# A two-layer trunk on one core: low halves of two weight chunks on VectorE, a longer distance between row sums, spread and turned row, odd heads' scores one product later, and values scaled in blocks

## The chip, the core and the metric

The kernel runs on one NeuronCore of a Trainium2 chip. The metric is the device time of one execution in microseconds (us); the time before is the median of three runs.

## What is computed

The reference has two decoder layers on a sequence of 512 tokens with 1024 channels. Both end in a SwiGLU feed-forward block; the first mixes tokens with dilated window attention in three head groups of eight heads, the second with a pooling mixer. The change touches the attention layer alone:

```python
def rmsnorm(x, g):
    y = xf * lax.rsqrt(jnp.mean(xf * xf, axis=-1, keepdims=True) + RMS_EPS)
    return (y * g.astype(jnp.float32)).astype(x.dtype)
...
    qkv = (h @ w_qkv).astype(jnp.float32).reshape(B, S, N_ATTN_GROUPS, 3, HEADS_PER_GROUP, HEAD_DIM)
...
    s = jnp.einsum('bnqhd,bnkhd->bnhqk', qb, kb) * (D ** -0.5)
    s = s + bias[None, None]
    p = jnp.exp(s - m)
    den = jnp.sum(p, axis=-1, keepdims=True)
    o = jnp.einsum('bnhqk,bnkhd->bnqhd', p / den, vb)
...
    wts = jax.nn.softmax(jnp.stack(lses, axis=0), axis=0)
    o = jnp.sum(wts[..., None] * o, axis=0).reshape(B, S, ATTN_WIDTH)
    return o.astype(h.dtype) @ w_out
```

## The kernel before

**High and low parts.** Every matrix operand is split into a high part in the type fp32r and a low part, the rest, and a product is three matmuls: high by high, high by low, low by high. `split` (lines 90 to 92) lets ScalarE write the high part and VectorE the low one by a subtraction. A plain chunk of weights (class `Plain`) can instead be "lean" (lines 144 to 148): ScalarE writes the high part, then its negative into the low part's place, and GpSimd issues a transfer that reads the chunk from HBM a second time and adds it there. Two chunks at the start, those of the third head group's query and key of head 0 (`w_qk`, line 241), are lean.

**Seven products.** Most other weights come as `Pair` units: Strassen's scheme with seven half-size products in place of eight. `Pair.load` (line 165) starts three loads on the SP queue (L169, L170, L171) and one on GpSimd's queue that adds a quarter onto the loaded first buffer (L172, line 172). The steps `blocks`, `sums`, `more` and `last` then split the parts "b", "s", "m" and "l"; `more` first makes its sums on VectorE (L188, L189), and every split has its high part at L91 on ScalarE and its low part at L92 on VectorE. Part "s" is made of the buffer onto which the accumulating transfer adds, so it cannot be split before that transfer lands. Loads stand in buffers `raw` (four) and `rawhalf` (two), split weights in `w` (five) and `half` (two); `pump` starts a load or split when its buffers are free. `seven` (line 465) computes such a unit (L456 to L458), `values12` (line 618) the values of two head groups for two heads at once (L632 to L634), and between their products run hooks, "behind(i)".

**The start.** A loop over eight blocks of channels loads input and first weights, and runs 96 matmuls (L927) for the first four query and key tiles. Meanwhile ScalarE and VectorE add up the squares of the input (L377, L379). Then, in the order of lines 930 to 970: `begin` starts the product of the first lean chunk with two of its eight blocks of channels; `prepare(0)` makes the sums of the input that Strassen's scheme wants (L576, L582 to L587, splits at L91 and L92); `rstd` (line 399) sums the squares over channels on TensorE (L406), forms the variance on VectorE (L409) and its power -1/2 on GpSimd in two halves (L412, tile `rcol`); `spread` (line 415) multiplies that column by an identity, so that every partition gets the row (L419, copied to `row` at L939); ScalarE reorders the row (L942, tile `line`) and four one-column matmuls turn it into columns (L944), from which and from `rcol` the scales `rk` are made (L946, L948). The eight blocks of the first lean chunk's product stand as two before the sums, three before the spread and three before the turned row; the whole product of the second chunk comes after. `evac` (line 608) moves the finished query and key tiles out (L613, L615).

**The heads.** Each head after the first computes its queries and keys by three calls of `seven`; an even head then computes the values of the first group by another call, an odd head those of the two other groups by `values12`. Hooks place the rest: `scores0` and `scores12` (scores of the first and of the two other groups), `scatter` and `merge` (one softmax over the groups), `turn0`, `turn12` (transposes of the weights), `output` (L843). `scores12` of an odd head reads the last key tile that L513 writes at the end of the third `seven`, and stands behind the first product of `values12`. At its end, `values12` scales the four blocks (classes) of its result by `rk` on ScalarE (L680), in four whole blocks.

**What sets the order.** The program is recorded and a scheduler orders each engine's instructions by its own estimates; on the chip each engine runs its list in that order and waits in place. So the order below is that of the built programs.

Of the kernel before, what the change touches and what calls it, by code (L numbers as in the profile page):

```python
# [18 lines left out]
KC = D // P  # L19
# [45 lines left out]
def trunk(ctx: ExitStack, tc: tile.TileContext, xT, xN, norms, w_first, w_qk, w_qkp, w_v0p, w_v12, w_out, w_outp, w_pair, w_down, w_dblock, w_pin, w_pgrp,  # L65
# [172 lines left out]

    for h in range(HEADS):
        if h == 0:  # L240
            plain(*[w_qk[u] for u in range(len(QK) - NF)], lean=True)
        for g in range(3):
            if h:
                pairs(w_qkp[3 * h - 3 + g])
        if h % 2 == 0:
            pairs(w_v0p[h // 2])
        else:
            pairs(w_v12[h // 2, 0], w_v12[h // 2, 1], shift=APART)
# [351 lines left out]
    with tc.tile_pool(name="opool", bufs=1) as opool:  # L600
        with tc.tile_pool(name="apool", bufs=1) as apool:
# [16 lines left out]
            def values12(after={}):  # L618


                t = apool.tile([P, NT, 4 * P], F32, name="v12")
                unit, = units.popleft()

                def product(name, half, key):
                    p = ps()
                    for a in range(2):
                        for k in range(K2):
                            wh, wl = (v[:, half * S + k % 2 * H2:half * S + (k % 2 + 1) * H2]
                                      for v in part(unit[k // 2], name).t)
                            mh, ml = (blk(v, a) for v in T[key, k])  # L630
                            o = both(p)[:, a]
                            nc.tensor.matmul(o, mh, wh, start=k == 0, stop=False)  # L632
                            nc.tensor.matmul(o, mh, wl, start=False, stop=False)  # L633
                            nc.tensor.matmul(o, ml, wh, start=False, stop=k == K2 - 1)  # L634
                        pump()
                    return p

                def done(name):
                    for u in unit:
                        u.w[name].done()  # L640

                def behind(i):
                    for f in after.get(i, ()):
                        f()

                def quarter(a, c):
                    return t[:, 2 * a:2 * a + 2, c * H2:(c + 1) * H2]

                m1 = product("b", 0, "11")
                first = scratch("first")  # L650
                nc.scalar.copy(first, m1)
                behind(0)
                m2 = product("b", 1, "21")
                nc.vector.tensor_add(quarter(0, 0), both(m2), both(first))
                done("b")
                behind(1)
                m5 = product("s", 0, "1")
                behind(2)
                m7 = product("s", 1, "3")
                done("s")  # L660
                behind(3)
                m6 = product("m", 0, "2")
                u2 = scratch("sums")
                nc.vector.tensor_add(u2, m6, first)
                u3 = scratch("sums")
                nc.vector.tensor_add(u3, m7, u2)
                nc.vector.tensor_sub(quarter(1, 1), both(m5), both(u3))
                behind(4)
                m3 = product("m", 1, "22")
                done("m")  # L670
                rest = scratch("first")
                nc.vector.tensor_add(rest, m3, u2)
                nc.vector.tensor_sub(quarter(1, 0), both(rest), both(m5))
                behind(5)
                m4 = product("l", 0, "4")
                done("l")
                nc.vector.tensor_sub(quarter(0, 1), both(m4), both(u3))
                behind(6)
                for r in range(NT):
                    nc.scalar.activation(t[:, r], t[:, r], AF.Copy, scale=rk[:, 1, r:r + 1])  # L680
                return t

            VT = []
# [246 lines left out]
            square(0, KC - 1)  # L930
            nc.sync.dma_start(ident, ident_in)
            nc.sync.dma_start(const[:, :3 * G + P], consts[:, :3 * G + P])
            lead += begin(1, 0, range(2))
            prepare(0)
            rcol = rstd([acc[0]])
            lead[-1].add(range(2, 5))
            rows["row"] = apool.tile([P, S], F32, tag="row", name="row")
            rk = apool.tile([P, NT, NT], F32, name="rk")
            nc.scalar.activation(rows["row"], spread(rcol), AF.Copy)  # L939
            lead[-1].add(range(5, KC))  # L940
            p, line = ps(), scratch("line")
            nc.scalar.copy(line[:1].rearrange("p (x y z) -> p x y z", y=Y16, z=2), in_a_row(rows["row"][:1]))  # L942
            for b in range(NT):
                nc.tensor.matmul(p[:, b:b + 1], blk(line, b)[:1], ones[:1], start=True, stop=True)  # L944
            for i, scale in ((0, 1.0), (2, SCALE)):
                nc.scalar.activation(rk[:, i], p[:, :NT], AF.Copy, scale=scale)  # L946
                for t, c in enumerate(rcol):
                    nc.scalar.activation(rk[:, i + 1, t:t + 1], c, AF.Copy, scale=scale)  # L948

            def later(f, *a):  # L950
                return lambda: f(*a)
# [11 lines left out]
            for u in range(NF):  # L963
                evac(0, u, lead[u].p)
            prepare(2)
            lead += begin(1, 0, range(KC))
            prepare(3)
            for u in range(NF, len(QK)):
                evac(0, u, lead[u].p)
# [2 lines left out]
            for h in range(HEADS):  # L972
                for g in range(3 if h else 0):
                    for c in range(2):
                        QKV[h, g, c] = apool.tile([P, S], F32, name=f"qk{g}{c}")
                    seven(T, QKV[h, g, 0], QKV[h, g, 1], scratch, between(h, g), g == 0, rows["row"])
                if h == 1:
                    O = [opool.tile([P, 2, S], F32, tag=f"o{k}", name="o") for k in range(K2)]
                    o.extend(O[h % K2][:, h // K2] for h in range(HEADS))
                if h % 2 == 0:  # L980
                    VT[:] = [apool.tile([P, n], F32, tag=tag, name="vt")[:, :S] for tag, n in (("room", 2 * S), ("o0", S))]
                    seven(T, *VT, scratch, {0: [] if h else [later(scores0, h)], 3: [later(scores12, h)],
                                            6: [later(scatter, h)]}, True)
                elif h < HEADS - 1:
                    QKV[h // 2, 12, 2] = values12({0: [later(scores12, h)], 4: [later(scatter, h)]})
                else:
                    QKV[h // 2, 12, 2] = values12({0: [later(scores12, h)], 1: [later(halve, 0), later(halve, 1)],
                                                   2: [later(scatter, h), later(halve, 2), later(halve, 3)],
                                                   3: [later(merge, h)],
                                                   4: [later(give, ("t", k, 0)) for k in range(2)]  # L990
                                                   + [later(halve, 4), later(halve, 5)]})
# [527 lines left out]
```

## Time and profile before

| What | Value |
|---|---|
| median of three runs | 1200.92 us |
| the runs | 1200.90, 1200.92 and 1203.81 us |
| the profiled execution | 1201.55 us |
| span of its instructions | 1199.8 us |
| mean granted TensorE clock | 0.996 |
| TensorE (PE) busy | 1180.0 us, 98% |
| weight loads (PEld) busy | 1125.4 us, 94% |
| VectorE (DVE) busy | 993.6 us, 83% |
| ScalarE (ACT) busy | 753.5 us, 63% |
| GpSimd (POOL) busy | 174.4 us, 15% |
| DMA, mean | 176 GB/s |

PE, PEld, DVE, ACT and POOL are the profile's names for TensorE's matmuls, its weight loads, VectorE, ScalarE and GpSimd; SPq and POOLq are the queues that issue transfers. In the views below a row of the timeline gives start, duration, engine, line, operation, the tiles written and read, their shapes, and in brackets the idle time before with what ended it. A row of the view of waits gives the total, the number and the longest of the waits. L327 is line 327. One execution was profiled; the 1.75 us of it outside the span lie before the first or after the last instruction.

### The profile page before, as it was taken

What the parts mean: (1) busy time and instruction counts of PE and PEld (TensorE: products, weight loads), DVE (VectorE), ACT (ScalarE), POOL (GpSimd) and SP (SyncE); (2) the same over time, 40 slices, a digit from 0 to 9 for tenths busy, and PEclk for the clock granted to TensorE, in tenths of its full rate; (3) what the DMA queues carried; (4) which work ended last, traced back from release to release, by engine and by line L of the source; (5) the groups of instructions that cost most, each with busy time, mean ns of one, the idle gap of its engine ahead of it and who ended that gap; (6) DMA issues with size and microseconds to landing.
All of it is one profiled execution on the core that took longest, in us unless ns stands there. A gap on an engine that the chain in (4) does not pass through costs nothing.

```text
span 1199.8 us, 25528 instructions
## 1 busy us (share of the span) xinstructions
PE 1180.0 (98%) x10158; PEld 1125.4 (94%) x10158; DVE 993.6 (83%) x1745; ACT 753.5 (63%) x1343; POOL 174.4 (15%) x170
## 2 busy tenths in 40 slices
PE   8899999999999999999999999999999999999997
PEld 7699999999999989889999999988888999999997
DVE  6698888889878979599988998755879998898875
ACT  8574655647556567657766775685574775677653
POOL 2121111111121001311111111121131111111100
PEclk9899999999999999999999999999999999999999
DMA  8666666766666464976777777698685777777732
GB/s 278 157 158 163 166 154 153 167 169 141 167 179 149 138 205 118 256 154 164 193 195 200 191 194 195 188 270 213 146 179 105 197 192 191 198 202 190 193 98 71
DMA packets 85304, 211.00 MB, mean 176 GB/s; under 512 B 7984, under 2 KB 13248, under 8 KB 85184
## 3 DMA queue, kind: packets, MB, share of 16 engines
q1 hardware_dynamic: 53104, 145.63, 36.6%
q0 software_dynamic: 31792, 63.46, 31.8%
q8 instruction: 79, 1.29, 0.4%
q14 instruction: 41, 0.34, 0.1%
q10 hardware_dynamic: 288, 0.29, 0.1%
HBM read 207.24 MB, written 2.10 MB: 174 GB/s over the span
## 4 chain that ended last, share of the span: by engine, by line
PE 83%; DVE 7%; DMA 6%; issue 2%; ACT 1%; POOL 1%; DVEq 0%; SPq 0%; POOLq 0%; ACTq 0%
PE ps L456 19%; PE ps L458 18%; PE ps L457 18%; PE ps L324 6%; PE ps L327 6%; PE ps L325 6%; DMA raw<-w_v 2%; PE ps L843 2%; DVE w L92 2%; PE ps L632 2%; PE ps L634 2%; PE ps L633 2%; DMA raw<-w_v0p 1%; DMA raw<-w_outp 1%; DVE half L92 1%
## 5 line engine op out<-in xcount | busy, mean ns | idle before, releaser
L91 ACT ACTIVATE w<-raw 128x1024 fp32r<-128x1024 f32 x269 | 285.4, 1063 | 185.0 <-PE ps L458 89.1
L92 DVE TENSOR_TENSOR w<-raw,w 128x1024 fp32r<-128x1024 f32 x269 | 328.5, 1223 | 55.2 <-ACT w L91 50.9
L456 PE MATMUL ps<-far,w 128*128 128x256 f32 x896 | 246.5, 275 | 0.0
L457 PE MATMUL ps<-far,w 128*128 128x256 f32 x896 | 246.5, 275 | 0.0
L458 PE MATMUL ps<-far,w 128*128 128x256 f32 x896 | 246.4, 275 | 0.0
L456 PE MATMUL ps<-near,w 128*128 128x256 f32 x749 | 210.9, 282 | 0.0
L458 PE MATMUL ps<-near,w 128*128 128x256 f32 x749 | 207.0, 276 | 0.0
L457 PE MATMUL ps<-near,w 128*128 128x256 f32 x749 | 206.9, 276 | 0.0
L456 PEld LDWEIGHTS ps<-far,w 128*128 128x128 f32 x896 | 168.2, 188 | 0.1
L457 PEld LDWEIGHTS ps<-far,w 128*128 128x128 f32 x896 | 168.2, 188 | 0.1
L458 PEld LDWEIGHTS ps<-far,w 128*128 128x128 f32 x896 | 168.2, 188 | 0.0
L456 PEld LDWEIGHTS ps<-near,w 128*128 128x128 f32 x749 | 140.7, 188 | 0.5
L457 PEld LDWEIGHTS ps<-near,w 128*128 128x128 f32 x749 | 140.8, 188 | 0.0
L458 PEld LDWEIGHTS ps<-near,w 128*128 128x128 f32 x749 | 140.8, 188 | 0.0
L327 PE MATMUL ps<-near,w 128*128 128x512 f32 (+1 forms) x332 | 126.1, 380 | 5.3 <-DMA w<-w_qk 5.3
L324 PE MATMUL ps<-near,w 128*128 128x512 f32 (+1 forms) x332 | 127.0, 383 | 0.0
L325 PE MATMUL ps<-near,w 128*128 128x512 f32 (+1 forms) x332 | 125.7, 378 | 0.0
L172 POOL DMA_DIRECT2D raw<-w_pair x36 | 43.6, 1210 | 293.7 <-DMA raw<-w_pair 135.3
L327 PEld LDWEIGHTS ps<-near,w 128*128 128x128 f32 x332 | 62.8, 189 | 17.4 <-DMA w<-w_qk 5.7
L325 PEld LDWEIGHTS ps<-near,w 128*128 128x128 f32 x332 | 63.0, 190 | 11.5 <-DVE near L92 0.2
L324 PEld LDWEIGHTS ps<-near,w 128*128 128x128 f32 x332 | 62.8, 189 | 11.6 <-ACT near L91 0.4
L188 DVE TENSOR_TENSOR raw<-raw 128x512 f32<-128x512 f32 x87 | 59.5, 684 | 10.7 <-DMA raw<-w_v0p 7.8
(340 smaller groups left out, 2739.3 us busy)
## 6 DMA issues: line engine op xcount, KB each, us to landing
raw<-w_pair SPq DMA_DIRECT2D x80, 512.0 KB, 4.9
raw<-w_qkp SPq DMA_DIRECT2D x42, 512.0 KB, 4.7
raw<-w_pair POOLq DMA_DIRECT2D x36, 512.0 KB, 7.6
raw<-w_dblock SPq DMA_DIRECT2D x32, 512.0 KB, 4.7
raw<-w_qkp POOLq DMA_DIRECT2D x21, 512.0 KB, 7.7
rawhalf<-w_pair SPq DMA_DIRECT2D x36, 256.0 KB, 5.1
raw<-w_v SPq DMA_DIRECT2D x16, 512.0 KB, 4.2
raw<-w_dblock POOLq DMA_DIRECT2D x16, 512.0 KB, 7.5
```

The costliest lines, as they stand in the source:

```text
L91: nc.scalar.activation(hi, v, AF.Copy)
L92: nc.vector.tensor_tensor(lo, v, hi.bitcast(F32), op=OP.subtract)
L172: nc.gpsimd.dma_start(self.b.rearrange("p (a c) -> p a c", a=2), self.src[:, None, 3 * n:].to_broadcast([P, 2, n]), accum_op=OP.add)
L188: nc.vector.tensor_add(a[:, :n], a[:, :n], b[:, :n])
L324: nc.tensor.matmul(self.p[:, cols], w[0][:, s], mh[:, cols], start=self.done == 0, stop=False)
L325: nc.tensor.matmul(self.p[:, cols], w[0][:, s], ml[:, cols], start=False, stop=False)
L327: nc.tensor.matmul(self.p[:, cols], w[1][:, s], mh[:, cols], start=False, stop=self.done == self.n)
L456: nc.tensor.matmul(dst, w.t[0][:, c], th, start=k == 0 and not on, stop=False, skip_group_check=on)
L457: nc.tensor.matmul(dst, w.t[0][:, c], tl, start=False, stop=False, skip_group_check=on)
L458: nc.tensor.matmul(dst, w.t[1][:, c], th, start=False, stop=k == n - 1, skip_group_check=on)
L632: nc.tensor.matmul(o, mh, wh, start=k == 0, stop=False)
L633: nc.tensor.matmul(o, mh, wl, start=False, stop=False)
```

## The change

It has four parts.

1. The two chunks of `w_qk` are no longer lean: their low parts come from a subtraction on VectorE (L92), and the two accumulating transfers (L148) go.
2. At the start the sums of squares (L406) come directly behind the 96 matmuls, then the whole product of the first chunk (24 matmuls), the spread, six of eight blocks of the second chunk's product (18 matmuls), the turned row and the last two blocks (6 matmuls). No product of a whole chunk is left behind the turned row.
3. In odd heads `scores12` and `scatter` move one product further on; in the last head `scatter` and `merge` stay where they were, and two of the splits of finished heads (`halve`) change places.
4. `values12` scales its result in smaller pieces as they are ready: the first half of the columns of blocks 0 and 1 and the whole of blocks 2 and 3 ahead of the last product, the second half of blocks 0 and 1 behind it.

```diff
-            plain(*[w_qk[u] for u in range(len(QK) - NF)], lean=True)
+            plain(*[w_qk[u] for u in range(len(QK) - NF)])
...
+                def scale(classes, c, n=1):
+                    for r in classes:
+                        v = t[:, r, c * H2:(c + n) * H2]
+                        nc.scalar.activation(v, v, AF.Copy, scale=rk[:, 1, r:r + 1])
...
                 behind(5)
+                scale(range(NT // 2), 0)
+                scale(range(NT // 2, NT), 0, 2)
                 m4 = product("l", 0, "4")
...
-                for r in range(NT):
-                    nc.scalar.activation(t[:, r], t[:, r], AF.Copy, scale=rk[:, 1, r:r + 1])
+                scale(range(NT // 2), 1)
...
-            lead += begin(1, 0, range(2))
+            rcol = rstd([acc[0]])
             prepare(0)
-            rcol = rstd([acc[0]])
-            lead[-1].add(range(2, 5))
+            lead += begin(1, 0, range(KC))
             rows["row"] = apool.tile([P, S], F32, tag="row", name="row")
             rk = apool.tile([P, NT, NT], F32, name="rk")
             nc.scalar.activation(rows["row"], spread(rcol), AF.Copy)
-            lead[-1].add(range(5, KC))
-            p, line = ps(), scratch("line")
+            line = scratch("line")
             nc.scalar.copy(line[:1].rearrange("p (x y z) -> p x y z", y=Y16, z=2), in_a_row(rows["row"][:1]))
+            lead += begin(1, 0, range(6))
+            p = ps()
             for b in range(NT):
                 nc.tensor.matmul(p[:, b:b + 1], blk(line, b)[:1], ones[:1], start=True, stop=True)
...
+            lead[-1].add(range(6, KC))
...
             prepare(2)
-            lead += begin(1, 0, range(KC))
             prepare(3)
...
-                    QKV[h // 2, 12, 2] = values12({0: [later(scores12, h)], 4: [later(scatter, h)]})
+                    QKV[h // 2, 12, 2] = values12({1: [later(scores12, h)], 5: [later(scatter, h)]})
                 else:
-                    QKV[h // 2, 12, 2] = values12({0: [later(scores12, h)], 1: [later(halve, 0), later(halve, 1)],
+                    QKV[h // 2, 12, 2] = values12({0: [later(halve, 0)], 1: [later(scores12, h), later(halve, 1)],
```

Lines behind the change have other numbers in the changed kernel: L412 stays, but L939, L942, L944, L948 of the start become L944, L946, L950, L954, and L680 becomes L652.

GpSimd's list at the start, from the first bias (L705) to the first accumulating transfers of head 1, before:

```order
7 L705 TENSOR_SCALAR b_518<-const 128x320
8 L708 TENSOR_SCALAR b_520<-const 128x128
9 L708 TENSOR_SCALAR b_520<-const 128x32
10 L148 DMA w<-w_qk 128x1024
11 L172 DMA raw<-w_v0p 128x2x512
12 L148 DMA w<-w_qk 128x1024
13 L172 DMA raw<-w_qkp 128x2x512
14 L412 TENSOR_TENSOR rcol<-var,nhalf 128x2 x2
```

The same list in the changed kernel:

```order
7 L711 TENSOR_SCALAR b_516<-const 128x320
8 L714 TENSOR_SCALAR b_518<-const 128x128
9 L714 TENSOR_SCALAR b_518<-const 128x32
10 L172 DMA raw<-w_v0p 128x2x512
11 L172 DMA raw<-w_qkp 128x2x512
12 L412 TENSOR_TENSOR rcol<-var,nhalf 128x2 x2
```

The transfer onto `w_v0p`, the first unit of `seven`, is now the first that this queue issues; the power at L412 still stands behind that onto the next unit.

ScalarE's list at the start, from the scales that read `rcol` to the reordered row (`half`, `near`, `w`, `t` and `tx` are high parts, `room` the scaled input), before:

```order
44 L948 ACTIVATE rk<-rcol 128x1 x6
45 L91 ACTIVATE w<-raw 128x1024
46 L948 ACTIVATE rk<-rcol 128x1 x2
47 L91 ACTIVATE near<-temp 128x512
48 L91 ACTIVATE t<-temp 128x512
49 L939 ACTIVATE row<-ps 128x512
50 L576 ACTIVATE room<-x,nrm 128x512
51 L942 COPY line<-row 1x512
```

In the changed kernel:

```order
39 L954 ACTIVATE rk<-rcol 128x1 x8
40 L91 ACTIVATE half<-rawhalf 128x512
41 L91 ACTIVATE near<-temp 128x512
42 L91 ACTIVATE w<-raw 128x1024
43 L91 ACTIVATE t<-temp 128x512
44 L576 ACTIVATE room<-x,nrm 128x512 x2
45 L91 ACTIVATE w<-raw 128x1024
46 L944 ACTIVATE row<-ps 128x512
47 L91 ACTIVATE tx<-temp 128x512
48 L946 COPY line<-row 1x512
```

Between the scales and the row there are now a half chunk, two operand splits, two weight splits and two scaled inputs, and one more split ahead of the reordering.

VectorE's list in the first odd head, from the multiplication that writes the last key tile (L513) to the scattering, before:

```order
128 L513 TENSOR_TENSOR qk_1087<-ps,row 128x512
129 L746 SCALAR_TENSOR_TENSOR s_1227<-ps,rk,b_993 128x160 x4
130 L748 TENSOR_REDUCE st<-s_1227 128x4
131 L749 TENSOR_SCALAR nm<-st 128x4
132 L654 TENSOR_TENSOR v_1199<-ps,first 128x2x256
133 L92 TENSOR_TENSOR w<-raw,w 128x1024
134 L759 TENSOR_TENSOR far<-st,place 128x64
```

In the changed kernel:

```order
127 L513 TENSOR_TENSOR qk_1085<-ps,row 128x512
128 L659 TENSOR_TENSOR v_1197<-ps,first 128x2x256
129 L92 TENSOR_TENSOR w<-raw,w 128x1024
130 L752 SCALAR_TENSOR_TENSOR s_1251<-ps,rk,b_991 128x160 x4
131 L92 TENSOR_TENSOR w<-raw,w 128x1024
132 L754 TENSOR_REDUCE st<-s_1251 128x4
133 L188 TENSOR_TENSOR raw<-raw 128x512
134 L755 TENSOR_SCALAR nm<-st 128x4
135 L189 TENSOR_TENSOR raw<-raw 128x512
136 L765 TENSOR_TENSOR far<-st,place 128x64
```

The first sum of `values12` (L654, now L659) and a low part come ahead of the four biased scores (L746, now L752).

## The prediction

> **What bounds the kernel now.** First the view of waits for TensorE over the whole execution, since the summary gives that engine 98%: total, number and longest of each wait in us (the idle start is left out).
>
> ```profile
> PE ps L327 <- DMA w<-w_qk: 5.3, 1, 5.3
> PE ps L743 <- DVE qk L513: 1.6, 2, 0.9
> PE ps L944 <- ACT line L942: 1.5, 1, 1.5
> ...
> PE ps L843 <- ACT v L680: 1.3, 1, 1.3
> ...
> PE ps L843 <- ACT t L810: 1.0, 1, 1.0
> PE ps L419 <- POOL rcol L412: 0.8, 2, 0.7
> ```
>
> These are all the waits of the bounding engine, 11.5 us, and the change aims at each but one. Next the table by stretches: busy time per engine, then granted clock, DMA share and GB/s.
>
> ```profile
> 32.00:39.00 7.00, 5.61 (x43) 4.19 (x44) 2.40 (x4) 2.41 (x4) 0.00 (x0) 0.51 1.12 229
> ...
> 80.00:100.00 20.00, 20.00 (x253) 19.83 (x252) 18.66 (x32) 10.62 (x20) 3.19 (x3) 1.00 0.55 150
> ```
>
> From 32 to 39 TensorE got 0.51 of its clock and worked 5.6 us, so at the full clock it would have needed some 2.8 us less: call it 2.5, as its one-column matmuls gain little. From 80 to 100 it never stops, with VectorE at 18.7 of 20. Third, the timeline of the start, in order of time.
>
> ```profile
> 19.17 1.45 POOL L708 TENSOR_SCALAR b<-const 128x128 f32<-128x128 f32 x2
> ...
> 22.22 1.07 POOL L148 DMA_DIRECT2D w<-w_qk  x1 [1.60 <-ACT w L146]
> 22.98 1.59 POOL L172 DMA_DIRECT2D raw<-w_v0p  x1
> ...
> 27.48 0.39 PE L324 MATMUL ps<-near,w 128*128 128x512 f32 x1
> ...
> 33.40 0.80 PE L327 MATMUL ps<-near,w 128*128 128x512 f32 x1 [5.30 <-DMA w<-w_qk]
> ...
> 36.59 1.06 ACT L91 ACTIVATE w<-raw 128x1024 fp32r<-128x1024 f32 x1 [7.28 <-PE ps L406]
> ...
> 37.80 1.22 DVE L92 TENSOR_TENSOR w<-raw,w 128x1024 fp32r<-128x1024 f32 x1
> ...
> 38.94 0.15 DVE L409 TENSOR_SCALAR var<-ps 128x4 f32<-128x4 f32 x1
> ...
> 41.24 0.71 PE L419 MATMUL ps<-ident,rcol 128*128 128x128 f32 x4 [0.19 <-POOL rcol L412]
> ...
> 45.57 1.05 PE L944 MATMUL ps<-ones,line 1*128 1x1 f32 x8 [1.53 <-ACT line L942]
> ...
> 46.55 0.50 PE L324 MATMUL ps<-near,w 128*128 128x512 f32 x1
> ...
> 52.13 0.28 PE L456 MATMUL ps<-near,w 128*128 128x256 f32 x1
> ...
> 56.45 0.28 PE L456 MATMUL ps<-near,w 128*128 128x256 f32 x1
> ```
>
> Two chains meet here. TensorE is ready for the first lean chunk at 27.5 and gets its low part at 33.4. The second chain is the longer: the transfer onto `w_v0p`, issued at 22.98, lands at 36.59 (the high half at L91 starts there; the releaser named, L406, had been done, so it was the transfer); its low half ends at 39.0, and the variance (L409) stands behind that in VectorE's list. Then come the power, the spread's second half at 41.24, the turned row at 45.57, 24 matmuls from 46.55 and the first of the seven products at 52.13.
>
> **The change, part by part.** *Lean off.* The low part that TensorE waited for now needs ScalarE's high halves, which by the order start where the old ones did, and two subtractions on VectorE of 1.22 us (row 37.80). Both of ScalarE's writes of the first chunk were over by 22.22, where L148 stops waiting for them; the subtraction can follow the first of them and should be done by 25, ahead of 27.5. So the wait of 5.3 goes, and with it the slow clock. The cost, 2.4 us of VectorE, falls where it waited: it worked 2.4 of 7 us from 32 to 39. ScalarE loses two writes.
>
> *What is late next.* VectorE's new list still has the low part of "s" ahead of the variance, so the landing of the accumulating transfer, A, sets the second chain. GpSimd's list now starts it behind the biases: 19.17 + 1.45 = 20.6, not 22.98, as the idle ahead of L148 was for ScalarE; its own load had come by then, since L172 followed L148 without a wait. It has no other accumulating transfer ahead of it. How long it takes is the disputed term. Times from issue to landing, min, median and max, for the two of L148 and then for L172 in the first 120 us:
>
> ```profile
> DMA to landing us min/median/max: 11.1/13.0/14.9
> DMA to landing us min/median/max: 6.7/7.9/13.5
> ```
>
> The longest of the second row is this very transfer before, behind another one. Ends: 20.6 + 6.7 = 27.3 and 20.6 + 13.5 = 34.1. Its nearest rows are the median (28.5), which has quieter stretches in it, and the 11.1 of the transfer that was first in the queue (31.7), which met the plain loads of the same stretch; I take 30.0 between. The Trainium skill (DMA: Bandwidth & Descriptors, "Anatomy of one DMA — SWDGE (gpsimd) path") puts such a transfer at 2.0 us plus its bytes by 436 GB/s, by which 512 KB would take an estimated 3.2 us, A would be 23.8 and TensorE alone would set the start. The trace disagrees: its shortest is 6.7.
>
> From A to the spread's second half nothing changes: 41.24 - 36.59 = 4.65. Of the queues moved past, the power at L412 stands behind GpSimd's issue for the next unit, done before 34 if that unit's load takes no longer than before. From there to the turned row ScalarE's list is longer. Its pieces are:
>
> ```profile
> 41.22 0.48 ACT L948 ACTIVATE rk<-rcol 128x1 f32<-128x1 f32 x4 [0.61 <-POOL rcol L412]
> ...
> 43.26 0.62 ACT L91 ACTIVATE t<-temp 128x512 fp32r<-128x512 f32 x1
> ...
> 43.79 0.57 ACT L939 ACTIVATE row<-ps 128x512 f32<-128x512 f32 x1
> ...
> 44.88 0.65 ACT L942 COPY line<-row 1x512 f32<-1x512 f32 x1
> ...
> 46.05 1.04 ACT L91 ACTIVATE w<-raw 128x1024 fp32r<-128x1024 f32 x1
> ...
> 49.48 1.32 ACT L576 ACTIVATE room<-x,nrm 128x512 f32<-128x512 f32 x2
> ```
>
> Six scales behind the second half of `rcol` (0.7); four splits of 512 columns at 0.62 (half, near, t, tx); two weight splits at 1.04; two scaled inputs, 1.32; row 0.57 and line 0.65: 7.8, less 0.1 of overlap at each of some eight seams, as 43.26 + 0.62 passes 43.79: 7.1, where before it was 45.57 - 41.24 = 4.3. TensorE covers only 18 matmuls of it: (52.13 - 46.55) / 24 = 0.23 each, 4.2, and 0.5 of the spread. So it still waits some 2.4 us at the turned row. Behind that stand 1.0 (46.55 - 45.57) and 6 matmuls, 1.4, not 24. The seven products start at A + 4.65 + 7.1 + 1.0 + 1.4 = A + 14.1: at 44.1 for A = 30.0, 8.0 earlier than 52.13. The ends of A give 10.7 and 3.9. TensorE itself needs, from 27.5, 48 matmuls (11.2), the turned row (1.0), spread (1.3) and sums (0.6): 41.6, a gain of 10.5 at most.
>
> The clock: the waits left are 0.5 at the spread and 2.4 at the turned row. Before, 1.53 there with another 0.8 just ahead left it at 1.00, and 5.3 brought 0.51; 2.4 lies between, nearer the first. The Trainium skill (TensorE: Matmul & The Clock Gate, "HAM oscillation — how this bites in real kernels") forbids idle gaps over some 3.4 us; by that rule, with which both rows agree, no loss follows here.
>
> *Odd heads and scaling.* The rows of the last head:
>
> ```profile
> 412.30 0.40 PE L743 MATMUL ps<-qk,qk 128*32 128x32 f32 x24 [0.77 <-DVE qk L513]
> ...
> 419.37 0.23 DVE L759 TENSOR_TENSOR far<-st,place 128x64 f32<-128x64 f32 x1
> 421.54 0.33 PE L771 MATMUL ps<-far,const 128*128 128x64 f32 x2
> ...
> 432.21 1.06 ACT L91 ACTIVATE w<-raw 128x1024 fp32r<-128x1024 f32 x1 [4.39 <-DMA raw<-w_outp]
> ...
> 434.11 1.72 PE L843 MATMUL ps<-t,v 128*128 128x128 f32 x14
> 435.73 2.54 ACT L680 ACTIVATE v<-v,rk 128x512 f32<-128x512 f32 x4
> 437.10 2.61 PE L843 MATMUL ps<-t,v 128*128 128x128 f32 x16 [1.27 <-ACT v L680]
> ...
> 445.71 1.54 PE L843 MATMUL ps<-t,v 128*128 128x128 f32 x11 [0.96 <-ACT t L810]
> ```
>
> A product lies between L513 and the scores now, so the two waits at L743 go: 1.6. In the last head ScalarE's eight scalings of the scores stood behind the split of 432.21 that waits for a transfer; in the new list they precede it, and the whole blocks follow it at once: 433.3 + 2 x 0.65 = 434.6, before TensorE reaches them at 435.8. The wait of 1.3 goes. What follows is the chain to L810, which starts earlier on both engines; of its 1.0 I count half. Against this, L771 had 421.54 - 419.60 = 1.9 in hand, while the scores of the last head now come a product later and its hook stays: a wait of 0 to 1.0, counted as 0.2, since ScalarE's two splits that stood ahead of the exponentials now run earlier. Sum 1.6 + 1.3 + 0.5 - 0.2 = 3.2, between 0.6 (the first alone, less 1.0) and 3.9. VectorE and ScalarE do the same work there but for 2 us of ScalarE over all heads, which has 37% to spare.
>
> Together 8.0 + 3.2 = 11.2. The profiled execution took 1201.55 (its span and 1.75 around it) and would take 1190.35; the median of the runs lies 0.63 lower: 1200.92 - 11.2 = 1189.7. A measurement of this kernel can tell some 0.3% (3.6 us) from no change.
>
> **The rivals.** *TensorE sets the start (B).* The transfer lands by 27, or ScalarE's queue fits better: 10.5 + 3.9 = 14.4, 1186.5. For it: the queue has lost two transfers; against: DMA shares of 1 through that stretch. *The transfer is no quicker (C).* Its 13.5 us came from the plain loads, not from L148: 3.9 + 3.2, 1193.8. For it: the 11.1 of the first one. *The clock falls at the turned row (D).* A wait of 2.4 beside the one-column matmuls is enough: 2.5 lost, 1192.2; with C 1196.3. *The start's gain is used up (E).* VectorE, with 18.7 of 20 from 80 to 100 and 2.4 us more to do, becomes the bound: 3.2 are left, 1197.7, within 0.3%. Against it: the low half done at 39.0 (row 37.80) is first used at 56.45, so the split weights lie 17 us ahead. *Slower (F).* In ScalarE's new list the row stands behind the split of the next unit's "b", whose load now starts later, as its buffer is held until VectorE has subtracted. A landing at L puts the seven products at L + 4.9; nominally L is under 39. With 2.5 for the clock the whole is slower by 0.3% from L = 52.13 + 3.2 + 3.6 - 2.5 - 4.9 = 51.5, some 27 us after its issue; no transfer in the rows above took over 14.9.
>
> **How the numbers follow.** The forecast has 0.46, B 0.16, C 0.17, D 0.10, E 0.07, F 0.04. Forecast, B, C and D are faster by over 0.3%: 0.89; E is 0.07 of no difference; F 0.04. The range leaves out E and F: up to 1196.3, C with D; down to 1185.5, 1 us under B, as the starts of matmuls around the listed waits lie some 0.2 further apart than these say.
>
> **What would show it.** Right: no wait at L327, the clock at 1.00 from 25 on, the transfer onto `w_v0p` landing at 28 to 32, the variance 2.35 behind it, a wait of 2 to 3 us at the turned row, the first seven products at 44; no wait at L743 nor for the scaled values; TensorE without new gaps between 45 and 400. A landing at 34 is C; 0.5 in the clock between 38 and 50 is D; new waits of TensorE for VectorE between 50 and 100 are E. I am wrong if the seven products start at 44 and the time falls by less than 6, or if they start after 49.

## The result and the profile after

| | before | after |
|---|---|---|
| median, four runs of each on one chip | 1200.95 us | 1187.91 us |
| lowest and highest | 1200.90, 1203.81 | 1187.28, 1192.83 |
| ratio, with its 95% interval | | 0.9895 [0.9865, 0.9925] |
| the profiled execution, its span | 1201.55, 1199.8 | 1192.83, 1191.1 |

The kernel became 13.0 us faster; the forecast was 1189.7 with a range from 1185.5 to 1196.3. The execution that the profiler took is the longest of the four; the others lie between 1187.28 and 1187.94. So a second profile of the same kernel (the first experiment, 1188.24) stands beside it below. Of the executions below two ran slow, one of e3 (1308.48, clock 0.849) and one of e11 (1686.9, clock 0.654); the medians count them, the ratios do not.

The first page line of after shows the same work (VectorE again 993.6) with TensorE's share at 99%. The view of TensorE's waits, second fence, has four rows.

```profile
PE 1177.6 (99%) x10158; PEld 1124.8 (94%) x10158; DVE 993.6 (83%) x1747; ACT 752.8 (63%) x1349; POOL 174.2 (15%) x168
```

```profile
PE ps L419 <- POOL rcol L412: 2.8, 2, 2.6
PE ps L950 <- ACT line L946: 2.2, 1, 2.2
PE ps L911 <- DVE idle L908: 1.2, 1, 1.2
PE ps L933 <- ACT w L925: 0.6, 1, 0.6
```

The last two lie ahead of and in the loop over the input, so 5.0 us are left of the 11.5 of before. The waits for the low part of a lean chunk (L327), for the last key tile (L743, now L749), for the scaled values (L680, now L652) and for the transposed weights (L810, now L816) are all gone. What is left stands at the spread (L419) and at the turned row (L950). The timeline of after's start:

```profile
22.67 1.38 POOL L172 DMA_DIRECT2D raw<-w_v0p  x1 [1.12 <-DVE sq L379]
...
33.23 1.06 ACT L91 ACTIVATE w<-raw 128x1024 fp32r<-128x1024 f32 x1 [5.45 <-issue]
...
35.47 0.16 DVE L409 TENSOR_SCALAR var<-ps 128x4 f32<-128x4 f32 x1
...
36.87 0.71 PE L419 MATMUL ps<-ident,rcol 128*128 128x128 f32 x4 [2.56 <-POOL rcol L412]
37.77 0.71 PE L419 MATMUL ps<-ident,rcol 128*128 128x128 f32 x4 [0.19 <-POOL rcol L412]
...
44.78 1.05 PE L950 MATMUL ps<-ones,line 1*128 1x1 f32 x8 [2.18 <-ACT line L946]
...
48.12 0.42 PE L456 MATMUL ps<-near,w 128*128 128x256 f32 x1
```

The transfer onto `w_v0p` lands at 33.23 (the split at L91 follows it), 10.5 after its issue, and the variance, the second half of the spread and the turned row follow 2.2, 4.5 and 11.6 behind it. In the repeat of the same kernel the same rows stand like this:

```profile
21.11 1.38 POOL L172 DMA_DIRECT2D raw<-w_v0p  x1 [0.57 <-DVE temp L582]
...
28.62 1.06 ACT L91 ACTIVATE w<-raw 128x1024 fp32r<-128x1024 f32 x1 [1.85 <-PE ps L406]
...
33.58 1.05 PE L419 MATMUL ps<-ident,rcol 128*128 128x128 f32 x8
...
40.50 1.05 PE L950 MATMUL ps<-ones,line 1*128 1x1 f32 x8 [1.75 <-ACT line L946]
...
42.97 0.28 PE L456 MATMUL ps<-near,w 128*128 128x256 f32 x1
...
60.12 0.41 PE L777 MATMUL ps<-far,const 128*128 128x64 f32 x2 [0.94 <-PE ps L456]
```

Here the transfer took 7.5, landed at 28.62, and the spread no longer waits: TensorE is busy with the first chunk until it gets there. The row follows 11.9 behind the landing, so the later chain is much the same. Ahead of the landing, the issue at L172 came in both profiles 0.7 behind the landing of the plain load onto the same buffer (L169, by the DMA view: 16.80 + 5.2 = 22.0 in the first, 15.79 + 4.6 = 20.4 in the repeat). The table by stretches of after (columns as before) has one stretch at half clock, behind the two waits of the late start:

```profile
25.00:32.00 7.00, 7.00 (x62) 5.59 (x61) 4.19 (x6) 2.78 (x5) 0.00 (x0) 1.00 0.88 231
...
46.20:49.60 3.40, 3.40 (x13) 2.93 (x12) 3.40 (x8) 1.93 (x5) 0.00 (x0) 0.50 0.54 135
80.00:100.00 20.00, 20.00 (x253) 19.83 (x253) 17.05 (x27) 9.13 (x18) 3.20 (x3) 1.00 0.57 145
```

Where the time came from is read by putting the same matmul of the traces beside each other: the first of `values12` of the first and of the last odd head, and one in the feed-forward block after attention. First before, then after:

```profile
97.75 0.28 PE L632 MATMUL ps<-w,near 128*128 128x256 f32 x1
...
407.92 0.28 PE L632 MATMUL ps<-w,near 128*128 128x256 f32 x1
...
538.39 0.28 PE L456 MATMUL ps<-far,w 128*128 128x256 f32 x1
```

```profile
94.25 0.28 PE L632 MATMUL ps<-w,near 128*128 128x256 f32 x1
...
403.21 0.28 PE L632 MATMUL ps<-w,near 128*128 128x256 f32 x1
...
529.69 0.28 PE L456 MATMUL ps<-far,w 128*128 128x256 f32 x1
```

The lead of after is 4.0 at the first of the seven products (52.13 against 48.12), 3.5 at 97.75, 4.7 at 407.92 and 8.7 at 538.39, and it stays there to the end (the spans differ by 8.7). In the repeat the four leads are 9.2, 8.1 (89.66), 9.3 (398.60) and 13.3 (525.12). So the start brought 3.5 in the one execution and 8.1 in the other, and the heads 5.2 in both, 4.0 of it in the last head.

### The profile page after: what moved, and what is told of

Its sections match the earlier page's. It is cut to its first block, busy times and chain, and to the rows that moved or that the text cites. A ratio compares the mean times of both kernels' runs of the same rounds, so it can differ in the third digit from the quotient of the medians.

```text
span 1191.1 us, 25533 instructions
## 1 busy us (share of the span) xinstructions
PE 1177.6 (99%) x10158; PEld 1124.8 (94%) x10158; DVE 993.6 (83%) x1747; ACT 752.8 (63%) x1349; POOL 174.2 (15%) x168
## 4 chain that ended last, share of the span: by engine, by line
PE 94%; ACT 2%; issue 1%; DMA 1%; DVE 0%; POOL 0%; SPq 0%; DVEq 0%; POOLq 0%; ACTq 0%
PE ps L456 21%; PE ps L458 21%; PE ps L457 21%; PE ps L324 6%; PE ps L325 6%; PE ps L327 6%; PE ps L849 2%; PE ps L632 2%; PE ps L634 2%; PE ps L633 2%; PE ps L725 1%; PE ps L745 1%; DMA x<-xT 1%; DMA raw<-w_v0p 1%; ACT w L91 0%
## 5 line engine op out<-in xcount | busy, mean ns | idle before, releaser
L91 ACT ACTIVATE w<-raw 128x1024 fp32r<-128x1024 f32 x271 | 286.6, 1062 | 160.9 <-PE ps L458 91.2
L92 DVE TENSOR_TENSOR w<-raw,w 128x1024 fp32r<-128x1024 f32 x271 | 330.7, 1222 | 55.3 <-ACT w L91 51.0
L327 PE MATMUL ps<-near,w 128*128 128x512 f32 (+1 forms) x332 | 125.5, 378 | 0.0
L172 POOL DMA_DIRECT2D raw<-w_pair x36 | 43.5, 1210 | 297.3 <-DMA raw<-w_pair 139.5
L327 PEld LDWEIGHTS ps<-near,w 128*128 128x128 f32 x332 | 62.5, 188 | 11.7
```

Source lines behind the costliest of these rows:

```text
L91: nc.scalar.activation(hi, v, AF.Copy)
L92: nc.vector.tensor_tensor(lo, v, hi.bitcast(F32), op=OP.subtract)
L172: nc.gpsimd.dma_start(self.b.rearrange("p (a c) -> p a c", a=2), self.src[:, None, 3 * n:].to_broadcast([P, 2, n]), accum_op=OP.add)
L327: nc.tensor.matmul(self.p[:, cols], w[1][:, s], mh[:, cols], start=False, stop=self.done == self.n)
```

## The experiments

The theory: the start hangs on the landing of the transfer onto `w_v0p` and gains most of the time; the order of the heads takes away the waits at L743, L680 and L810. The rivals: the gain is in the heads; TensorE or the distance between the sums and the row sets the start; the landing doesn't depend on the queue. Ratios are to the kernel before on the same chip, with 95% intervals; its medians there were 1200.19 (e1 to e4), 1200.82 (e5 to e8) and 1199.85 (e9 to e12).

**The change again** (`e1_after_again`), no edit.

> The changed kernel again, unaltered. Its profiled execution took 1192.83 us, the other three 1187.3 to 1187.9. Theory (the landing of the first accumulating transfer sets the start): where this profile shows a time near 1188, that transfer lands at 28 to 30 us instead of 33.2, the seven products start some 14 us behind it, at 43 to 44 instead of 48.1, and the heads' part of the trace is the same to 0.3 us. Rival (the clock): the landing is the same at 33 and the profiled execution differs from the others only by the half clock from 46.2 to 49.6 us, worth 1.7 us at most, so the seven products start at 47 to 48 again.

Measured: 1188.07, 0.9898 [0.9886, 0.9911], from 1187.70 to 1188.97. Its start is the second timeline above. The landing came 4.6 earlier, and the profiled executions differ by 4.6; the heads gain the same 5.2 in both, as expected.

**Part 1 alone** (`e2_plain_only`), in the kernel before:

```diff
-            plain(*[w_qk[u] for u in range(len(QK) - NF)], lean=True)
+            plain(*[w_qk[u] for u in range(len(QK) - NF)])
```

> Of the change the first part alone: low halves of the two chunks on VectorE, order of the start as before. Theory: the accumulating transfer lands some 4 to 7 us earlier, as it is first in its queue, and the seven products start 15.5 us behind the landing as before; the wait at L327 and the half clock go but are worth nothing by themselves, since the landing sets the chain. Gain 4 to 7 us: 1194 to 1197. Rival (order): the gain comes from the longer stretches of products between sums, spread and turned row; this kernel gains under 2 us: 1199 to 1201.

Measured: 1194.45, 0.995 [0.9935, 0.9965]: 5.7 faster, over six runs that scatter from 1191.82 to 1198.41. The clock stays at 1.00 and the wait at L327 is gone. The transfer onto `w_v0p`, issued at 21.16, lands at 28.96, and the seven products start at 44.62, 15.7 behind it and 7.5 earlier than before; 0.7 of this is lost again in the heads (a lead of 6.8 behind them).

**Part 2 alone** (`e3_order_only`): the start's new order in the kernel before, with both chunks lean.

```diff
-            lead += begin(1, 0, range(2))
+            rcol = rstd([acc[0]])
             prepare(0)
-            rcol = rstd([acc[0]])
-            lead[-1].add(range(2, 5))
+            lead += begin(1, 0, range(KC))
...
+            lead += begin(1, 0, range(6))
...
+            lead[-1].add(range(6, KC))
```

> Of the change the second part alone: sums first and the longer distances, both chunks still lean. Theory: the transfer onto the first pair still stands behind a lean one and lands at 36 to 37; the seven products start 14.1 us behind it, not 15.5: gain 1 to 2 us, 1199 to 1200. Rival (order): the sums no longer wait for the lean chunk, so the row comes early and 5 to 8 us are gained: 1193 to 1196.

Measured: 1200.58, 1.0001 [0.9992, 1.0010]. Moving the sums, the spread and the row apart brings nothing by itself. In the profiled execution, its shortest (1199.44), the transfer lands at 33.87, 2.7 earlier than before and than was expected, and the seven products start 14.0 behind it, 4.2 earlier; but the end is only 2.1 earlier. The lead falls to 2.9 by 97.75, with the clock at half from 45.5 to 48.9, and by 0.9 more in the heads. Two rows of its waits:

```profile
PE ps L944 <- ACT line L940: 2.7, 1, 2.7
PE ps L743 <- DVE qk L513: 2.6, 4, 0.9
```

The first is the row, now too close behind ScalarE's longer list; the second shows where the heads take back some of an earlier start, at L743, while the old hooks stand: 2.6 in four waits here, 2.6 in three with part 1 alone, 1.6 in two before.

**Parts 3 and 4 alone** (`e4_heads_only`), in the kernel before: the hooks and the pieces of the scaling.

```diff
+                scale(range(NT // 2), 0)
+                scale(range(NT // 2, NT), 0, 2)
...
-                    QKV[h // 2, 12, 2] = values12({0: [later(scores12, h)], 4: [later(scatter, h)]})
+                    QKV[h // 2, 12, 2] = values12({1: [later(scores12, h)], 5: [later(scatter, h)]})
```

> Of the change the third and fourth parts alone: odd heads' scores one product on and values scaled in blocks, the start as before. Theory: all four waits of the heads go with their restarts (two at L743, those for the scaled values and for the last head's transposes), 4.5 to 5.2 us as the trace of the changed kernel suggests: 1195.7 to 1196.4. Rival (my prediction's sum): 3.2, 1197.7. Rival (they only showed at the changed start): under 2, 1199 or more.

Measured: 1195.00, 0.9959 [0.9947, 0.9972]: 5.2 faster, with the start as before (the seven products at 51.83 against 52.13). That is the heads' share in the whole change too, so the forecast of 3.2 was too small, and the other 6.9 of the first batch (1195.00 - 1188.07) belong to the start. Parts 1 and 2 were not run together without the others; the 6.9 is a difference.

**Part 3 alone** (`e5_scores_only`), only the hooks of the diff above and the changed place of `halve`.

> Of the change the third part alone: odd heads' scores one product on. Theory: exactly the waits at L743 go, 0.85 and 0.77 us with restarts of 0.2 each in heads 3 and 7 and 0.3 each in heads 1 and 5: 2.3 to 2.7 us, so 1197.5 to 1198; the waits of the last head at L843 stay. Rival: in the last head the merge now waits for the later scores and takes 0.5 to 1.0 back, 1198.5 or more, with a wait at L771.

Measured: 1195.02, 0.9954 [0.9938, 0.9970]: 5.8 faster, more than twice what was expected and by the median as much as both parts. In the profiled execution the heads gain 4.8, and 2.7 of its lead came from a start that happened to be earlier. TensorE's waits, all of them:

```profile
PE ps L327 <- DMA w<-w_qk: 2.6, 1, 2.6
PE ps L419 <- POOL rcol L412: 1.7, 2, 1.5
PE ps L905 <- DVE idle L902: 1.2, 1, 1.2
```

L743 and the last head's waits for L680 and L810 are gone without any change to the scaling. ScalarE's timeline in the last head shows what moved:

```profile
422.69 1.07 ACT L91 ACTIVATE w<-raw 128x1024 fp32r<-128x1024 f32 x1
423.66 1.37 ACT L785 ACTIVATE s<-s,co 128x160 f32<-128x160 f32 x4
424.93 1.37 ACT L788 ACTIVATE s<-s,co 128x160 f32<-128x160 f32 x4
426.21 1.05 ACT L91 ACTIVATE w<-raw 128x1024 fp32r<-128x1024 f32 x1
427.16 2.55 ACT L680 ACTIVATE v<-v,rk 128x512 f32<-128x512 f32 x4
```

The eight scalings of the scores (L785, L788) now stand ahead of the split that used to wait 4.39 for `w_outp` (432.21 before), and the whole-block scaling follows in time. That split waits no more either: the transfer that it needs is issued at 416.50 and lands at 424.6, where before it was 422.55 and 432.2. Of these 7.6 us 3.5 are the earlier arrival at this head (404.40 against 407.92); the rest came with the hooks, as two weight splits ahead of it now start at 409.46, not 415.68. The new order and the earlier landing were not tried apart; both come of part 3.

**Part 4 alone** (`e9_scale_only`): the pieces of the scaling, with the old hooks.

> Of the change the fourth part alone: values scaled in blocks, all else as before. Theory (the waits of the last head went by ScalarE's order, which the third part moved: the scalings of the scores now stand ahead of the split that waits for a transfer): this kernel keeps both splits ahead of them, the wait at L843 for the scaled values shrinks by the 1.2 us that two whole blocks take less or stays, the waits at L743 stay; gain under 1.5 us, 1199 to 1200.8. Rival (the blocks did it, as my prediction summed): the waits for the scaled values and for the transposes go, 2.3 to 2.9, 1197.5 to 1198.

Measured: 1201.60, 1.0012 [1.0001, 1.0023] over twelve runs: nothing gained, perhaps a microsecond or two lost (in the profiled execution the heads lose 0.5). ScalarE's list in the last head, then two rows of TensorE's waits:

```profile
432.30 1.06 ACT L91 ACTIVATE w<-raw 128x1024 fp32r<-128x1024 f32 x1 [4.29 <-DMA raw<-w_outp]
...
435.83 2.12 ACT L652 ACTIVATE v<-v,rk 128x512 f32<-128x512 f32 x4
```

```profile
PE ps L749 <- DVE qk L513: 2.7, 3, 1.2
...
PE ps L849 <- ACT t L816: 1.8, 1, 1.8
```

The scalings still stand behind the split that waits, 0.4 shorter in all; the wait for the values is gone from the list, and that for the transposes behind them grew from 1.0 to 1.8.

**One chunk lean, in the changed kernel** (`e6_first_chunk_lean`, `e7_second_chunk_lean`). The two edits are the same line for the one and the other chunk:

```diff
-            plain(*[w_qk[u] for u in range(len(QK) - NF)])
+            plain(w_qk[0], lean=True)
+            plain(w_qk[1])
```

> The changed kernel with the first chunk lean again (the second is not). Its accumulating transfer stands ahead of that onto the first pair in GpSimd's queue. Theory (the landing of the pair's transfer sets the start): it lands 3 to 6 us later than in the changed kernel, at 32 to 36, and the seven products start 14 to 15 us behind it, at 47 to 50, where they started at 43.0 in the repeated changed kernel; TensorE also waits for the chunk's low part at about 33. Loss against the changed kernel 4 to 7 us: 1192 to 1195. Rival (traffic: each lean transfer costs the same share of DMA time): half of what the first part alone gave, 2.5 to 3 us, as much as with the other chunk lean.

> The changed kernel with the second chunk lean again (the first is not). Its transfer stands behind that onto the first pair. Theory: the pair's transfer lands as in the changed kernel or up to 1 us later, and the loss is under 2 us, unless the chunk's low part lands behind 35, when TensorE is ready for it. 1188 to 1190. Rival (traffic): the same loss as with the first chunk lean, 2.5 to 3 us or more.

Measured: 1193.63, 0.9942 [0.9921, 0.9962] with the first chunk lean, 1190.12, 0.9910 [0.9892, 0.9927] with the second: 5.7 and 2.2 above the change. The seven products start at 47.33 and 44.35, against 42.97 in the repeat. GpSimd's issues and the landing, first the one, then the other:

```profile
21.37 1.06 POOL L148 DMA_DIRECT2D w<-w_qk  x1 [1.61 <-ACT w L146]
22.13 1.58 POOL L172 DMA_DIRECT2D raw<-w_v0p  x1
...
33.98 1.06 ACT L91 ACTIVATE w<-raw 128x1024 fp32r<-128x1024 f32 x1 [7.46 <-issue]
```

```profile
20.73 1.38 POOL L172 DMA_DIRECT2D raw<-w_v0p  x1 [0.73 <-DVE temp L583]
23.34 0.90 POOL L148 DMA_DIRECT2D w<-w_qk  x1 [1.22 <-ACT w L146]
...
30.86 1.06 ACT L91 ACTIVATE w<-raw 128x1024 fp32r<-128x1024 f32 x1 [4.62 <-issue]
```

The bytes are the same; only which of the two transfers is first differs. Behind a lean chunk's transfer the one onto `w_v0p` is issued 1.4 later and takes 11.8; ahead of it, it takes 10.1. So the place in the queue counts, 3.5 us by the medians. That the traffic of the second transfer counts too is likely from the 2.2, but 10.1 lies within the 7.1 to 10.5 that the transfer took with no lean chunk at all, so the trace doesn't show it.

**No transfer onto the first pair** (`e11_first_pair_not_added`). The accumulating transfer of `w_v0p` is left out (one of the four quarters that its sums need is missing), in the changed kernel; all else stays.

```diff
-            nc.gpsimd.dma_start(self.b.rearrange("p (a c) -> p a c", a=2),
-                                self.src[:, None, 3 * n:].to_broadcast([P, 2, n]), accum_op=OP.add)
+            if self.added:
+                nc.gpsimd.dma_start(self.b.rearrange("p (a c) -> p a c", a=2),
+                                    self.src[:, None, 3 * n:].to_broadcast([P, 2, n]), accum_op=OP.add)
```

> The changed kernel without the accumulating transfer onto the first pair, which leaves a quarter out of that unit's sums. Theory (its landing holds VectorE's list, and with it the variance): the variance is formed at 28.5 to 31 instead of 30.9 to 35.5, the power then waits for GpSimd's issue at L177 for the next pair at about 30 to 32; the seven products start at 42 to 43.5 in any execution and the runs lie within 1 us of each other, 1187 to 1188.2. Rival (the plain loads of the start make the scatter): the runs scatter as those of the changed kernel did, up to 1192.

Measured: 1186.04, 0.9883 [0.9866, 0.9900], a microsecond under what was expected and close to the 1186.5 of rival B. Three of its four executions lie between 1185.83 and 1186.15, where the change had 1187.28 to 1192.83. TensorE's waits are these, and its start (the lines lie five later):

```profile
PE ps L916 <- DVE idle L913: 1.2, 1, 1.2
PE ps L782 <- PE ps L461: 0.3, 1, 0.3
```

```profile
38.80 1.05 PE L955 MATMUL ps<-ones,line 1*128 1x1 f32 x8
...
41.26 0.28 PE L461 MATMUL ps<-near,w 128*128 128x256 f32 x1
```

Without the landing TensorE never waits between the loop over the input and the seven products: the first of the seven products comes at 41.26, where the prediction's sum for TensorE alone had put it at 41.6. What the landing still costs the changed kernel is 42.97 - 41.26 = 1.7 in the repeat and 6.9 in the first profile.

**The turned row elsewhere** (`e8_turned_row_later`, `e12_turned_row_behind_chunk`, `e10_turned_row_whole_scaling`). In e8 the second chunk's product is whole ahead of the row, and the row's four matmuls with the scales `rk` that come of them stand behind the first of the seven products:

```diff
-            lead += begin(1, 0, range(6))
-            p = ps()
-            for b in range(NT):
-                nc.tensor.matmul(p[:, b:b + 1], blk(line, b)[:1], ones[:1], start=True, stop=True)
+            lead += begin(1, 0, range(KC))
...
-            lead[-1].add(range(6, KC))
+            def turned():
+                p = ps()
+                for b in range(NT):
+                    nc.tensor.matmul(p[:, b:b + 1], blk(line, b)[:1], ones[:1], start=True, stop=True)
+                for i, scale in ((0, 1.0), (2, SCALE)):
+                    nc.scalar.activation(rk[:, i], p[:, :NT], AF.Copy, scale=scale)
...
-                    seven(T, *VT, scratch, {0: [] if h else [later(scores0, h)], 3: [later(scores12, h)],
+                    seven(T, *VT, scratch, {0: [] if h else [turned, later(scores0, h)], 3: [later(scores12, h)],
```

> The changed kernel with the turned row behind all of the second chunk's product and the first of the seven products, just ahead of the first scores. Theory: the wait left at the turned row, 1.8 us in the repeated changed kernel and 2.2 in the other profile, goes; nothing else is late, so 1.5 to 2 us are gained: 1186 to 1186.6. Rival: ScalarE is what paces the start, and what was waited for at the turned row is waited for at the scores or at the next split operands: no gain, 1188.

Measured: 1185.70, 0.9871 [0.9853, 0.9888]. No wait behind the loop over the input is left:

```profile
PE ps L911 <- DVE idle L908: 1.2, 1, 1.2
PE ps L933 <- ACT w L927: 0.2, 1, 0.2
```

In e12 the row only moves behind the second chunk's product (`range(6)` becomes `range(KC)`, and nothing is left behind the row).

> The changed kernel with all eight blocks of the second chunk ahead of the turned row, none behind it. Theory: 6 matmuls, 1.4 us, of the wait of 1.8 to 2.2 are covered: 1186.4 to 1187. Rival (what is covered here is waited for at the first scores): 1188.

Measured: 1187.03, 0.9892 [0.9879, 0.9905]: the row waits no more, but the interval doesn't tell it from the change. Its profiled execution (1188.41, the longest of four) again had a transfer of 10.5, which landed at 32.11. In e10 the scaling of e8 is put back to four whole blocks.

> The kernel with the turned row later, with values scaled in four whole blocks at the end as before the change. Theory (the blocks are worth nothing beside the third part): the same time within 0.5 us, 1185.2 to 1186.2, and no wait of TensorE at L843. Rival: the wait for the scaled values is back, 1.3 to 2.4 us, 1187 to 1188.

Measured: 1185.59, 0.9880 [0.9867, 0.9893]: the medians show no worth of part 4 beside part 3. The traces show a little: in e10 TensorE waits 0.2 at L843 for the scaled values in the first odd head and loses 0.8 around it, and the heads gain 4.2 where in e8 they gain 5.2. With the 4.8 of e5 against the 5.2 of e4, part 4 is worth 0.4 and 0.9 in two pairs of traces, which these medians can't tell from nothing.

Both e8 and e10 beat the change, by some 2 us: their eight executions (1184.70 to 1186.01) are all shorter than its eight (1187.28 to 1192.83). Beside the repeat, the profile of e8 is 3.5 shorter: 1.8 is the wait at the row, 0.9 a wait at L777 that e8 doesn't have, and 0.65 an earlier landing (27.97).

## Why the prediction was right, step by step

**Lean off.** Right. TensorE does not wait at L327, the clock is 1.00 from 25 on, VectorE does two subtractions more at a place where it had waited. Part 1 alone, with the earlier landing that it brings, is worth 5.7.

**The landing.** Right as the term that decides, with a spread wider than one number can hold. The forecast of 30.0 was an issue at 20.6 and 9.4 of transfer. The repeat had 21.1 and 7.5; the first profile 22.7 and 10.5, which is rival C in its own terms (landing at 34, 1193.8; it took 1192.83). That the place in the queue matters, against rival C, is shown by e6 and e7. "Its own load had come by then" was half a microsecond too early, as the issue followed that load in both. In the first profile the load itself landed 1.6 later, 1.0 of it already in its issue; why the transfer then took 3.0 longer is open. Of the six profiles in which no lean chunk shares the queue, four landed between 27.5 and 29.0 (e1, e2, e8, e10) and two at 32.1 and 33.2 (e12, after). So 30.0 was a middle of two groups and near no landing that was profiled. The Trainium skill's 2.0 us plus bytes by 436 GB/s (DMA: Bandwidth & Descriptors, "Anatomy of one DMA — SWDGE (gpsimd) path"), an estimated 3.2 us, is contradicted again: of the seven profiled executions with this transfer first in its queue, the shortest (e8) took 7.1 (issue at 20.82, landing at 27.97).

**The chain behind it.** Right. Forecast 14.1 from the landing to the seven products; 14.35 in the repeat, 14.9 in the first profile, where the half clock added 0.9, 14.0 in e3, 13.4 and 13.5 in e6 and e7. From the spread's second half to the row 7.0 (37.77 to 44.78) against 7.1, from ScalarE's list alone. The wait at the row was 1.8 and 2.2 against 2.4 (the sign named was 2 to 3); at the spread 0 and 2.6 against 0.5, as the landing came. Rival F, a load that comes late to the splits ahead of the row, did not show.

**The start's sum.** Forecast 8.0. The repeat had 9.2 at the seven products and 8.1 at 97.75: 0.94 goes at L777 (L771 before) in the first head, where TensorE now arrives ahead of its operand; this is a new gap, which the signs of the prediction had excluded. So 8.0 met 8.1 by luck: the landing came 1.4 earlier than forecast, and L777 took most of it back. By the medians of e1 and e4 it is 6.9. Rival E, in which all of the start is used up, is out: TensorE has no wait for VectorE between 50 and 100, and VectorE went down to 17.0 of 20 from 80 to 100. That e2 and e3 give 5.7 and nothing, but 6.9 is left for both, goes with the waits at L743, which grow by 1.0 in each when the start moves ahead under the old hooks; the interval of e2, some 1.8 us either way, is wider than the difference.

**The clock.** The step "2.4 lies nearer the first, no loss" held in the repeat and failed in the first profile, with 3.4 us at half clock behind waits of 2.56 and 2.18: TensorE's matmuls from the row to the seven products took 2.36 there and 1.49 in the repeat. It is 0.9, and 1.4 us with the 0.5 by which the lead shrank from 4.0 to 3.5 behind it, not the 2.5 of rival D.

**The heads.** This is the term that was mis-sized: forecast 3.2, measured 5.2 in e4 and in both traces. L810 went whole (1.0, not 0.5), L771 cost nothing in the odd heads (not 0.2), and 1.3 is in no row of the view of waits, which listed 3.9 in all. By place, from the same matmuls beside each other: 1.2 came between 97.75 and 407.92, 0.9 of it in the fourth head, where 0.85 was listed, and 0.15 each in the second and sixth, where nothing was. The last head gave 4.0, where 3.0 was listed: 0.6 within `values12` (0.8 listed) and 3.4 behind it (2.2 listed).

**The scaling in blocks.** The step that named it was half right. The prediction put the wait of 1.3 down to score scalings behind a split that waits, and said they would precede it; that was so, and came from the hooks (e5), which moved the split's landing as well. "The whole blocks follow it at once" gave the scaling in blocks a share in this wait that it does not have beside the hooks: e5 loses the wait without it. By the medians e9 and e10 show no gain of it; what the traces of e4, e5, e8 and e10 leave to it is under 1.0.

## What to carry to other kernels

A step that waits in place holds all that is behind it in that engine's list: when a wait goes away after a change, look for what now stands ahead of the blocked instruction, and when the thing it waits for came, before crediting the edit that touches the waiting tile. A transfer on which a long chain hangs should be the first that its queue issues, and here an engine with idle time at that point was a cheaper place for a chunk's low part than the same queue. A chain of fixed steps behind a landing can be forecast to within a microsecond (13.4 to 14.9 against 14.1); the landing itself needs a range.

## What the runs showed of the hardware

The half clock is not decided by the length of one wait. With parts 3 and 4 alone a wait of 1.54 at the row was followed by 3.4 us at half clock; in e12 a wait of 2.2 at the spread was followed by none. Nor is it the sum of two close waits: in e5 waits of 1.52 and 0.19 at the two halves of the spread were followed by half clock from 39.1 to 42.5, and in e12 the same two were 2.21 and 0.20. The table by stretches, first of e4, then of e12:

```profile
45.50:48.90 3.40, 3.40 (x10) 2.62 (x9) 3.40 (x6) 2.62 (x5) 0.00 (x0) 0.50 0.86 150
```

```profile
36.00:46.00 10.00, 9.80 (x101) 8.22 (x104) 9.67 (x16) 9.09 (x22) 1.83 (x2) 1.00 0.90 232
```

The kernel before had 1.53 at the same place without a loss. The Trainium skill (TensorE: Matmul & The Clock Gate, "HAM oscillation — how this bites in real kernels") gives idle gaps of over some 3.4 us as the point; here the trace disagrees, since gaps of 1.5 to 2.6 were enough in some executions. Whether it is where a gap falls in the clock's own rhythm was not tested. A sign of such a rhythm is that in e4, e5 and e9, which have two half-clock stretches each, the starts lie 13.65, 6.83 and 13.65 apart, 4, 2 and 4 times the 3.41 that each lasts.

A transfer of the same bytes onto the same buffer took between 7.1 (e8) and 13.5 us (before) from issue to landing, in one and the same kernel 7.5 and 10.5. With the issue, which was 1.6 apart too, this is the 4.6 us between the two profiled executions of the changed kernel. Behind a lean chunk's transfer in the same queue it took 11.1 to 13.5 in six profiles; as the first of its queue 7.1 to 10.5 in seven.
